# Seven block products for eight in the up-projection of a two-layer encoder trunk, with the down-projection beside them

## The chip, the cores and the metric

The kernel runs on one core of a Trainium2 chip. Its time is the device time of one execution in microseconds (us), taken as the median of three runs. The profile is one further execution, with its own time. The engines are named as in the profile: PE is the matrix engine's multiplication, PEld its loading of the stationary operand, DVE the vector engine, ACT the scalar engine, POOL the GpSimd engine, SP the engine that issues most transfers.

## The reference

The trunk has two layers over 512 tokens of width 1024. Each layer is a mixer (attention or a matrix memory, with an output projection) and then a channel mixer, and this case is about the channel mixers alone:

```python
def causal_dwconv(x, w, b):          # width 3 along the tokens, one filter per channel
    ...
def conv_ffn(h, w_up, conv_w, conv_b, w_down):
    u, g = jnp.split(h @ w_up, 2, axis=-1)
    g = causal_dwconv(g, conv_w, conv_b)
    return (jax.nn.silu(g) * u) @ w_down

x = x + conv_ffn(rmsnorm(x, norm_ffn_g[l]), ffn_w_up[l], ffn_conv_w[l], ffn_conv_b[l], ffn_w_down[l])
```

`w_up` is 1024 x 5632 (an up half and a gate half of 2816 = 22 x 128 columns each), `w_down` is 2816 x 1024. All data are 32-bit floats.

## The kernel before

**Precision.** Every product is made of three matrix multiplications. A value t is split into a high part in the PE's reduced 32-bit format (a cast on ACT, line 129) and a low part t minus high (a subtraction on DVE, line 130). `mm3` (lines 162 to 164) then adds high by high, high by low and low by high in one PSUM bank.

**Layout.** The tokens lie along the free dimension. `xT` is the residual stream: eight tiles of 128 channels x 512 tokens. The input of the channel mixer is `act`, eight pairs (high, low) of `xT` times the norm's gain. The per-token factor of the norm, `norm.row`, is multiplied in afterwards.

**One hidden tile.** `ffn_hidden(l, j, act, norm)` makes hidden tile j of 22. `project` loads the 1024 x 128 weights of the gate (512 KB), splits them, and runs 8 x 3 multiplications of 128x128 by 128x512; the up half has the same. So a tile is 48 multiplications of 512 columns. From the gate's bank, DVE multiplies by the norm's row (line 632), ACT starts the convolution (line 634), DVE adds its other two taps (line 636), ACT applies Silu (line 639), DVE multiplies by the row (line 640) and by the up half (line 644), and the result is split into a pair.

**Chunks.** The 22 tiles come in chunks of 8, 8 and 6 (`CHUNKS`). After each chunk, the down-projection multiplies the chunk's pairs by the rows of `w_down` and adds to the residual (line 951 in layer 0, line 1152 in layer 1): 528 multiplications of 512 columns in a layer. Layer 1 does this part token-major (hidden tile stationary, weights moving), after 32 transposes of `xT` (`token_major`), which stand in its first chunk.

**Order and buffers.** A scheduler sets the order on each engine, save inside a block marked as manual, where PE, ACT and DVE keep the order in which the code is written. Each engine runs its own instructions strictly in order. Tiles come from rings with a number of buffers per tag: `wr`, `wh`, `wl` (raw weights, high and low part) three each, `u` 57, `t` eight, `pt` two; PSUM banks are `mm` three, `sc` three, `tr` two. `xspill` is a copy of the residual in device memory; `reload_x` reads it back.

Of the kernel before, what the change touches and what calls it, by code (L numbers as in the profile page):

```python
# [10 lines left out]
F32R = mybir.dt.float32r  # L11
I32 = mybir.dt.int32
AF = mybir.ActivationFunctionType
ALU = mybir.AluOpType
AX = mybir.AxisListType

P = 128
# [18 lines left out]
    (("fw0", 66), ("fb0", 22)),  # L36
    (("fw1", 66), ("fb1", 22)),
)
CHUNKS = ((0, 8), (8, 16), (16, 22))


def f(ap):
# [4 lines left out]
def trunk(  # L47
# [80 lines left out]
    def split(hi, lo, src, on_act=True, pinned=False):  # L128
        high = A.copy(hi, src) if on_act else V.tensor_copy(hi, src)  # L129
        low = V.tensor_tensor(out=lo, in0=src, in1=f(hi), op=ALU.subtract)  # L130
        if pinned:
            pin(high)
            pin(low)
# [27 lines left out]
    def mm3(o, lh, ll, rh, rl, first, last):  # L161
        nc.tensor.matmul(o, lh, rh, start=first, stop=False)  # L162
        nc.tensor.matmul(o, lh, rl, start=False, stop=False)  # L163
        nc.tensor.matmul(o, ll, rh, start=False, stop=last)  # L164
# [75 lines left out]
    class Norm:  # L240


        def __init__(self):
            self.acc = self.row = None
# [343 lines left out]
    class OutProjection:  # L588
# [30 lines left out]
    def ffn_hidden(l, j, act, norm):  # L619
        w = ffn_w_up[l]  # L620
        fw, fb = col[f"fw{l}"], col[f"fb{l}"]
        gate, up = project(w, DFF + j * P, act), project(w, j * P, act, "sc")
        og = ou = None
        if norm.row is None:
            both = pair_of(gate, up)
            weave(norm.finish(), both, 1)
            og, ou = run(both)
        else:
            og = run(gate)
        pre = sb("t", [P, S + 4])  # L630
        G.memset(pre[:, 0:2], 0.0)
        V.tensor_tensor(out=pre[:, 2 : S + 2], in0=og, in1=norm.row, op=ALU.mult)  # L632
        acc = sb("t", [P, S])
        A.activation(acc, pre[:, 0:S], AF.Identity, scale=fw[:, j : j + 1], bias=fb[:, j : j + 1])  # L634
        for c in (1, 2):
            V.scalar_tensor_tensor(  # L636
                acc, pre[:, c : c + S], fw[:, c * FT + j : c * FT + j + 1], acc, op0=ALU.mult, op1=ALU.add
            )
        A.activation(acc, acc, AF.Silu)  # L639
        V.tensor_mul(acc, acc, norm.row)  # L640
        if ou is None:
            ou = run(up)
        hid = sb("t", [P, S])
        V.tensor_tensor(out=hid, in0=ou, in1=acc, op=ALU.mult)
        hi, lo = sb("u", [P, S], F32R), sb("u", [P, S], F32R)
        split(hi, lo, hid)
        return hi, lo


    def pair(t):  # L650
# [286 lines left out]
    for ci, (j0, j1) in enumerate(CHUNKS):  # L937
        hid = []
        for j in range(j0, j1):
            hid.append(ffn_hidden(0, j, act, norm))  # L940
            if ci and len(reps) < BH:
                bias_rows()
        last = ci == len(CHUNKS) - 1
        if last:
            norm2, kvact, act = Norm(), [], []
        for j in range(KT):
            wh, wl = weights(rows(ffn_w_down[0], j * P, P, j0, j1), j1 - j0, P)
            o = ps("mm")
            for k in range(j1 - j0):
                mm3(o, wh[:, k, :], wl[:, k, :], *hid[k], k == 0, k == j1 - j0 - 1)  # L950
            V.tensor_add(xT[j], xT[j], o)  # L951
            if last:
                norm2.add(xT[j])
                kvact.append(scaled(xT[j], col["gkv"][:, j : j + 1]))
                act.append(scaled(xT[j], col["gmix"][:, 8 + j : 9 + j]))
                G.dma_start(xspill[j], xT[j])
    norm = norm2


# [163 lines left out]
    for ci, (j0, j1) in enumerate(CHUNKS):  # L1123
        hid = []
        for j in range(j0, j1):
            hid.append(ffn_hidden(1, j, act, norm))
            if ci == 0:
                token_major(j % TT, j // TT)
        last = ci == len(CHUNKS) - 1
        n = (j1 - j0) // 2  # L1130
        for hf in range(2):
            os_ = [ps(t) for t in (("mm", "mm", "mm", "sc") if hf == 0 else ("sc", "sc", "tr", "tr"))]
            ws = [None] * n
            groups = [(range(TT), (slice(0, S),))]
            if last and hf:

                groups = [((0, 1), (slice(0, S),)), ((2,), (slice(0, S),)), ((3,), (slice(0, MEM), slice(MEM, S)))]
            for Ts, pieces in groups:
                for c in pieces:
                    if c.start:  # L1140
                        os_[Ts[0]] = ps("mm")
                    for u in range(n):
                        if ws[u] is None:
                            ws[u] = weights(rows(ffn_w_down[1], hf * S, S, j0 + 2 * u, j0 + 2 * u + 2), 2, S)
                        wh, wl = ws[u]
                        for T in Ts:
                            for i in range(2):
                                k = 2 * u + i
                                lh, ll = (t[:, T * P : (T + 1) * P] for t in hid[k])
                                mm3(os_[T][:, c], lh, ll, wh[:, i, c], wl[:, i, c], k == 0, k == j1 - j0 - 1)  # L1150
                    for T in Ts:
                        V.tensor_add(xt[T][hf][:, c], xt[T][hf][:, c], os_[T][:, c])
                        if last:
                            add_squares(T, xt[T][hf][:, c])
                            if hf == 0:
                                V.tensor_mul(xt[T][0], xt[T][0], fgb[0])
                            elif c.stop == S:
                                final_norm(T)


# [44 lines left out]
```

## Time and profile before

| | |
|---|---|
| median of 3 runs | 1232.34 us (1232.07 to 1232.56) |
| profiled execution, its own time | 1232.33 us |
| its span, first to last instruction | 1230.5 us |
| granted PE clock | 0.999 of full speed |
| PE busy | 1219.2 us, 99% of the span |
| PEld busy | 1022.7 us, 83% |
| DVE busy | 807.4 us, 66% |
| ACT busy | 560.5 us, 46% |

The span is 1.8 us shorter than the execution's own time, and the profiled execution agrees with the median to 0.01 us. PE's busy time is the union of the rows of its multiplications; a row begins where the multiplication begins to stream and ends when its last result is through, so rows of successive multiplications overlap. What a multiplication costs in a row of many is therefore the distance between two starts, not the length of a row.

### The profile page before, as it was taken

How to read it: one execution, taken by the hardware profiler on the slowest of the kernel's cores; microseconds unless marked ns; L12 is line 12 of the kernel's file. 1: busy time of each engine (PE TensorE's matmuls, PEld its weight loads, DVE VectorE, ACT ScalarE, POOL GpSimd, SP SyncE). 2: the span in 40 equal slices, each digit the busy share in tenths (PEclk: the TensorE clock that was granted, in tenths of full speed). 3: DMA queues.
4: the chain of work that ended last, by engine and by line, in shares of the span. 5: the costliest groups of instructions: out<-in, count | busy, mean ns of one | idle time of the engine just before them, and what ended most of it. 6: DMA issues, size and time to landing. Idle time of an engine off the chain costs nothing.

```text
span 1230.5 us, 15552 instructions
## 1 busy us (share of the span) xinstructions
PE 1219.2 (99%) x5839; PEld 1022.7 (83%) x5839; DVE 807.4 (66%) x1427; ACT 560.5 (46%) x911; POOL 55.3 (4%) x155
## 2 busy tenths in 40 slices
PE   9999999999999999999999999999999999999997
PEld 8988888888888888888888888888888888888886
DVE  7877687787564466445688888987656255544555
ACT  4546576644332233223365677775334123322334
POOL 1300000000000011000011000000000000000000
PEclk9999999999999999999999999999999999999999
DMA  8634111333344344424263323243232333323321
GB/s 271 210 90 120 53 53 56 116 103 104 103 113 110 104 126 129 125 87 113 77 180 113 93 70 98 61 141 112 88 102 86 103 90 99 103 87 101 103 86 69
DMA packets 190301, 130.63 MB, mean 106 GB/s; under 512 B 6328, under 2 KB 177810, under 8 KB 190226
## 3 DMA queue, kind: packets, MB, share of 16 engines
q1 hardware_dynamic: 186130, 116.59, 31.7%
q0 software_dynamic: 4096, 13.05, 3.8%
q8 instruction: 46, 0.75, 0.3%
q14 instruction: 29, 0.24, 0.1%
HBM read 122.08 MB, written 11.47 MB: 109 GB/s over the span
## 4 chain that ended last, share of the span: by engine, by line
PE 95%; ACT 2%; DVE 1%; DMA 0%; issue 0%; SPq 0%; DVEq 0%; ACTq 0%
PE pmm L162 20%; PE pmm L163 19%; PE pmm L164 19%; PE psc L162 8%; PE psc L163 8%; PE psc L164 8%; PE psc L500 2%; PE ptr L164 1%; PE ptr L162 1%; PE ptr L163 1%; PE ptr L1029 1%; PE ptr L1050 1%; PE ptr L1051 1%; DMA u<-in_mem_dram 0%; PE ptr L569 0%; PE ptr L583 0%
## 5 line engine op out<-in xcount | busy, mean ns | idle before, releaser
L129 ACT CAST wh<-wr 128x1024 fp32r<-128x1024 f32 (+2 forms) x208 | 210.1, 1012 | 432.9 <-issue 178.1
L162 PE MATMUL pmm<-u,wh 128*128 128x512 f32 (+1 forms) x960 | 378.0, 394 | 0.0
L164 PE MATMUL pmm<-u,wl 128*128 128x512 f32 (+1 forms) x960 | 373.9, 390 | 0.0
L163 PE MATMUL pmm<-u,wh 128*128 128x512 f32 (+1 forms) x960 | 373.6, 389 | 0.1
L130 DVE TENSOR_TENSOR wl<-wr,wh 128x1024 fp32r<-128x1024 f32 (+2 forms) x208 | 243.9, 1173 | 98.3 <-ACT wh L129 97.7
L164 PEld LDWEIGHTS pmm<-u,wl 128*128 128x128 f32 x960 | 180.4, 188 | 36.6
L163 PEld LDWEIGHTS pmm<-u,wh 128*128 128x128 f32 x960 | 180.7, 188 | 33.1 <-DVE u L130 0.5
L162 PEld LDWEIGHTS pmm<-u,wh 128*128 128x128 f32 x960 | 180.6, 188 | 32.8
L162 PE MATMUL psc<-u,wh 128*128 128x512 f32 x368 | 143.6, 390 | 0.0
L164 PE MATMUL psc<-u,wl 128*128 128x512 f32 x368 | 143.3, 389 | 0.0
L163 PE MATMUL psc<-u,wh 128*128 128x512 f32 x368 | 143.2, 389 | 0.0
L632 DVE TENSOR_TENSOR t<-pmm,rb 128x512 f32<-128x512 f32 x44 | 30.5, 692 | 116.1 <-PE pmm L164 116.0
L163 PEld LDWEIGHTS psc<-u,wh 128*128 128x128 f32 x368 | 69.1, 188 | 14.2
L162 PEld LDWEIGHTS psc<-u,wh 128*128 128x128 f32 x368 | 69.1, 188 | 14.3
L164 PEld LDWEIGHTS psc<-u,wl 128*128 128x128 f32 x368 | 69.1, 188 | 14.2
L636 DVE SCALAR_TENSOR_TENSOR t<-t,cols,t 128x512 f32<-128x512 f32 x88 | 65.9, 749 | 3.4 <-ACT t L634 1.9
L639 ACT ACTIVATE t<-t 128x512 f32<-128x512 f32 x44 | 27.8, 632 | 83.3 <-DVE t L636 83.3
L951 DVE TENSOR_TENSOR u<-u,pmm 128x512 f32<-128x512 f32 x24 | 16.5, 688 | 56.8 <-PE pmm L164 56.7
L640 DVE TENSOR_TENSOR t<-t,rb 128x512 f32<-128x512 f32 x44 | 30.5, 693 | 29.8 <-ACT t L639 29.8
L162 PE MATMUL pmm<-wh,u 128*128 128x512 f32 (+3 forms) x128 | 45.8, 363 | 1.5 <-ACT wh L129 1.5
L163 PE MATMUL pmm<-wl,u 128*128 128x512 f32 (+3 forms) x128 | 46.0, 360 | 0.0
L164 PE MATMUL pmm<-wh,u 128*128 128x512 f32 (+3 forms) x128 | 45.5, 358 | 0.0
(261 smaller groups left out, 1609.0 us busy)
## 6 DMA issues: line engine op xcount, KB each, us to landing
wr<-in_ffn_w_up_dram SPq DMA_DIRECT2D x88, 512.0 KB, 3.8
wr<-in_ffn_w_down_dram SPq DMA_DIRECT2D x38, 512.0 KB, 3.7
wr<-in_a_w_in_dram SPq DMA_DIRECT2D x20, 512.0 KB, 3.7
wr<-in_w_kv_dram SPq DMA_DIRECT2D x12, 512.0 KB, 3.8
xspill<-u POOLq DMA_DIRECT2D x16, 256.0 KB, 2.6
u<-xspill SPq DMA_DIRECT2D x16, 256.0 KB, 4.8
wr<-in_b_w_in_dram SPq DMA_DIRECT2D x8, 512.0 KB, 4.2
rep<-in_b_rel_row_dram POOLq DMA_DIRECT2D x12, 320.0 KB, 4.7
```

What stands on the lines that cost most here:

```text
L129: high = A.copy(hi, src) if on_act else V.tensor_copy(hi, src)
L130: low = V.tensor_tensor(out=lo, in0=src, in1=f(hi), op=ALU.subtract)
L162: nc.tensor.matmul(o, lh, rh, start=first, stop=False)
L163: nc.tensor.matmul(o, lh, rl, start=False, stop=False)
L164: nc.tensor.matmul(o, ll, rh, start=False, stop=last)
L500: nc.tensor.matmul(o, a, b, start=first and i == 0, stop=i == 1)
L632: V.tensor_tensor(out=pre[:, 2 : S + 2], in0=og, in1=norm.row, op=ALU.mult)
L636: V.scalar_tensor_tensor(acc, pre[:, c : c + S], fw[:, c * FT + j : c * FT + j + 1], acc, op0=ALU.mult, op1=ALU.add)
L639: A.activation(acc, acc, AF.Silu)
L640: V.tensor_mul(acc, acc, norm.row)
L951: V.tensor_add(xT[j], xT[j], o)
L1029: nc.tensor.transpose(tp[:, b * P : (b + 1) * P], es[T, h][:, b * P : (b + 1) * P], ident)
```

## The change

Tiles 0 to 6 of each layer are made as before, apart from tiles 4 to 6, whose input already holds the norm's row and gain. From tile 7 on (`PLAIN`), gate and up half of one tile are one block product:

- The weights of a tile are four blocks: a11 and a12 (up half, first and second half of the 1024 rows), a21 and a22 (gate half). The input is four blocks as well: two halves of the channels by two halves of the tokens (256 columns each).
- Four sums of weight blocks are made per tile on DVE (line 845 of the new code): s1 = a21 + a22, s2 = s1 - a11, s3 = a11 - a21, s4 = a12 - s2. Four sums of input blocks per channel pair are made once in a layer (`forms`). The sums are split into high and low part like everything else.
- Seven products replace eight: a11, a12, a22, s1, s2, s3 and s4, each with one block or sum of the input. A product is 4 x 3 multiplications of 256 columns, so a tile is 84 multiplications of 256 columns. Two banks, r1 and r3, hold partial sums that several outputs share: ACT copies r1 out (lines 796, 802, 812, 819), then PE goes on adding to r1. DVE adds the pieces (lines 799, 813, 895).
- The block for tiles 7 to 21 (`later`, `step`) is a manual order of PE, ACT and DVE. Step j holds the products of tile j, the end of tile j-1 (`Tail`: the taps, Silu, gate times up, the split) and the weight sums and splits of tile j+1 (`Forms`).
- Inside each step up to tile 20, and beside the plain tiles 5 and 6, stand two down-projection products over four hidden tiles each (24 multiplications of 512 columns, lines as `down_products`): ACT copies the result out of PSUM (line 735) and POOL adds it to `xspill` in device memory with an accumulating transfer (line 736). This covers hidden tiles 0 to 15; `reload_x` then brings the residual back, and tiles 16 to 21 (`LAST`) go through the down-projection at the end as in the last chunk before. Both layers now write `xspill` in `OutProjection.finish` (line 619). Layer 1's tiles 0 to 15 are now channel-major, and its 32 transposes stand between the two halves of its last part.

```diff
-CHUNKS = ((0, 8), (8, 16), (16, 22))
+PLAIN, UNSCALED, GROUP, LAST = 7, 4, 4, 6
+H = S // 2
...
                 V.tensor_add(xT[j], xT[j], o)
+                pin(G.dma_start(xspill[j], xT[j]))
...
+        def forms(self):
+            for j in range(KT):
+                V.scalar_tensor_tensor(
+                    xT[j], xT[j], self.gain[:, j : j + 1], self.norm.row, op0=ALU.mult, op1=ALU.mult
+                )
+                hi, lo = sb("u", [P, S], F32R), sb("u", [P, S], F32R)
+                split(hi, lo, xT[j])
...
+        def down_products(self, q, i, w):
+            g, jj = divmod(q, KT // 2)
+            o = ps("tr")
+            c = slice(i * P, (i + 1) * P)
+            for k in range(GROUP):
+                mm3(o, w[0][:, k, c], w[1][:, k, c], *self.hid[GROUP * g + k], k == 0, k == GROUP - 1)
+            return 2 * jj + i, o
+        def add(self, j, o):
+            t = sb("t", [P, S])
+            A.copy(t, o)
+            G.dma_start(xspill[j], t, accum_op=ALU.add)
...
+        def products(self, o, w, act, first=False):
+            n = KT // 2
+            for k in range(n):
+                mm3(o[:, :H], w[0][:, k], w[1][:, k], *act[k], first and k == 0, k == n - 1, True)
...
+        def step(self, j, w, nxt, tail):
+            new = Tail(self, j)
+            then(tail, "last_block", "first_tap")
+            w.split_fourth()
+            r1, r2, new.r3 = ps("mm"), ps("mm"), ps("sc")
+            new.up, new.u3, new.pre = sb("t", [P, S]), sb("t", [P, S]), sb("t", [P, S])
+            self.products(r1, w.a11, self.b(0, 0), True)
+            A.copy(new.up[:, :H], r1[:, :H])
+            then(tail, "second_tap")
+            self.products(r2, w.a12, self.b(1, 0), True)
+            V.tensor_tensor(out=new.up[:, :H], in0=new.up[:, :H], in1=r2[:, :H], op=ALU.add)
+            then(tail, "third_tap")
+            self.products(r1, w.s2, self.t(2))
+            A.copy(new.up[:, H:], r1[:, :H])
+            then(nxt, "sums")
+            then(tail, "gated")
+            then(nxt, "split_second", "sum_third")
+            w.down_products(0)
+            self.products(new.r3, w.s1, self.t(1), True)
+            w.add_down(0)
+            then(tail, "split")
+            then(nxt, "split_up")
+            self.products(r1, w.s3, self.t(3))
+            A.copy(new.u3[:, :H], r1[:, :H])
+            V.tensor_tensor(out=new.pre[:, H:], in0=new.u3[:, :H], in1=new.r3[:, :H], op=ALU.add)
+            then(nxt, "split_sums")
+            w.down_products(1)
+            then(nxt, "sum_fourth")
+            w.add_down(1)
+            self.products(r1, w.a22, self.t(4))
+            A.copy(new.pre[:, :H], r1[:, :H])
+            then(nxt, "split_down", "split_gate")
+            self.products(new.r3, w.s4, self.b(1, 1))
```

The prediction speaks of two places in the program. The first is ACT in the steady part of layer 0. Before, one hidden tile (`wh` are cast weights, `t` the convolution, `u` the hidden tile's high part; the names in brackets are the engines or transfers waited for):

```order
L129 CAST wh_4452<-wr_4450 128x1024 [waits DMAHW2_49,PE_49,Activation_49]
L634 ACTIVATE t_4364<-t_4361,cols_783 128x512 [waits DVE_49,Pool_49]
L639 ACTIVATE t_4364<-t_4364 128x512 [waits DVE_49]
L129 CAST wh_4492<-wr_4490 128x1024 [waits DMAHW3_49,PE_49,Activation_49]
L129 CAST u_4403<-t_4401 128x512 [waits DVE_49]
```

After, from the last copy of r1 in one step into the next step:

```order
L819 COPY t_4591<-pmm_4586 128x256 [waits PE_49]
L133 CAST wh_4726<-wr_4577 128x1024 [waits DMAHW7_49]
L133 CAST u_4730<-pt_3326 128x512 [waits DMAHW6_49]
L652 ACTIVATE t_4755<-t_4591,cols_783 128x512 [waits DVE_49,Activation_49]
L133 CAST u_4757<-pt_3327 128x512 [waits DVE_49]
L796 COPY t_4764<-pmm_4761 128x256 [waits PE_49]
L907 ACTIVATE t_4755<-t_4755 128x512 [waits DVE_49,Activation_49]
L802 COPY t_4764<-pmm_4761 128x256 [waits PE_49]
L133 CAST u_4812<-pt_3327 128x512 [waits DVE_49]
L735 COPY t_4842<-ptr_4817 128x512 [waits PE_49]
```

Between two copies of r1 there are now casts of the next tile's weights and sums (lines 133) and the last tile's convolution (line 652), in one queue.

The second place is PE, where the third product (s2, in `u_4637`) follows the second (a12) into r1 (`pmm_4761`), and then POOL, with the accumulating transfers:

```order
L169 MATMUL pmm_4762<-u_3322,wl_4675 128x256
L167 MATMUL pmm_4761<-u_3365,u_4637 128x256 [waits Activation_49]
L168 MATMUL pmm_4761<-u_3366,u_4637 128x256
L169 MATMUL pmm_4761<-u_3365,u_4638 128x256
L167 MATMUL pmm_4761<-u_3415,u_4637 128x256
```

The product s2 waits for ACT's copy of r1 (line 796, above); before, a bank was not added to again after it had been read.

```order
L1220 DMA rep_4746<-in_b_rel_row_dram 128x640
L1222 DMA rep_4746<-maskf 64x64 [waits DMASW2_49,DMASW1_49]
L736 DMA xspill<-t_4842 128x512 [waits DMASW3_49,Activation_49]
L736 DMA xspill<-t_4885 128x512 [waits DMASW4_49,Activation_49]
L1220 DMA rep_4921<-in_b_rel_row_dram 128x640
L1222 DMA rep_4921<-maskf 64x64 [waits DMASW6_49,DMASW5_49]
```

In layer 0 the two accumulating transfers of a step stand in POOL's queue between the two transfers that prepare layer 1's bias rows, which stood between the hidden tiles before as well.

More of the change, by code (lines that the diff above doesn't have):

```diff
@@ L159, in rows, with mm3 @@
         return w[k0 * P : k1 * P, c0 : c0 + n].rearrange("(k p) c -> p k c", p=P)
[L161 to L164, printed above, removed]
+    def mm3(o, lh, ll, rh, rl, first, last, more=False):
+        nc.tensor.matmul(o, lh, rh, start=first, stop=False, skip_group_check=more)
+        nc.tensor.matmul(o, lh, rl, start=False, stop=False, skip_group_check=more)
+        nc.tensor.matmul(o, ll, rh, start=False, stop=last, skip_group_check=more)
     def project(w, c0, act, tag="mm"):
@@ L617, in finish @@
             return norm, acts
[L619 to L637, printed above, removed]
-            )
[L639 to L647, printed above, removed]
@@ new lines, in trunk, with __init__, halves, form @@
+    class Forms:
+        def __init__(self, mixer, j):
+            self.mixer, n = mixer, KT // 2
+            self.q = j - GROUP - 1
+            self.up, self.gate = mixer.load_pair(j)
+            self.raw_down = mixer.load_down(self.q) if self.q < 4 * n else None
+            self.s13 = mixer.s[:, :D].rearrange("p (a b) -> p a b", a=KT)
+            self.s24 = mixer.s[:, D : 2 * D].rearrange("p (a b) -> p a b", a=KT)
+        def halves(self, t):
+            n = KT // 2
+            return t[:, :n], t[:, n:]
+        def form(self, src):
+            hi, lo = (sb("u", [P, S], F32R).rearrange("p (a b) -> p a b", a=KT // 2) for _ in range(2))
+            split(hi, lo, src)
+            return hi, lo
+        def sub(self, o, x, y, op=ALU.subtract):
+            V.tensor_tensor(out=o, in0=x, in1=y, op=op)
+        def sums(self):
+            a21, a22 = self.halves(self.gate)
+            s1, s2 = self.halves(self.s13)[0], self.halves(self.s24)[0]
+            self.sub(s1, a21, a22, ALU.add)
+            self.sub(s2, s1, self.halves(self.up)[0])
+        def split_second(self):
+            self.s2 = self.form(self.halves(self.s24)[0])
+        def sum_third(self):
+            self.sub(self.halves(self.s13)[1], self.halves(self.up)[0], self.halves(self.gate)[0])
+        def split_up(self):
+            self.a11, self.a12 = zip(*(self.halves(t) for t in parts(self.up)))
+        def split_sums(self):
+            self.s1, self.s3 = zip(*(self.halves(t) for t in parts(self.s13)))
+        def sum_fourth(self):
+            s2, s4 = self.halves(self.s24)
+            self.sub(s4, self.halves(self.up)[1], s2)
+        def split_down(self):
+            if self.raw_down is not None:
+                self.down = parts(self.raw_down)
+        def split_gate(self):
+            self.a22 = self.form(self.halves(self.gate)[1])
+        def split_fourth(self):
+            self.s4 = self.form(self.halves(self.s24)[1])
+        def down_products(self, i):
+            if self.raw_down is not None:
+                self.o = self.mixer.down_products(self.q, i, self.down)
+        def add_down(self, i):
+            if self.raw_down is not None:
+                self.mixer.add(*self.o)
@@ new lines, in trunk, with __init__, last_block, first_tap @@
+    class Tail:
+        def __init__(self, mixer, j):
+            self.mixer, self.j = mixer, j
+        def last_block(self):
+            c = self.up[:, H:]
+            V.tensor_tensor(out=c, in0=c, in1=self.r3[:, :H], op=ALU.add)
+        def first_tap(self):
+            self.acc = sb("t", [P, S])
+            self.mixer.last_tap(self.j, self.acc, self.pre)
+            self.taps = self.mixer.taps(self.j, self.acc, self.pre)
+        def second_tap(self):
+            next(self.taps)
+        def third_tap(self):
+            next(self.taps)
+            A.activation(self.acc, self.acc, AF.Silu)
+        def gated(self):
+            V.tensor_tensor(out=self.acc, in0=self.up, in1=self.acc, op=ALU.mult)
+        def split(self):
+            self.mixer.keep(self.acc)
@@ new lines, in channel_mixer @@
+    def channel_mixer(l, act, norm, gain, beside):
+        mixer = ChannelMixer(l, act, norm, gain, beside)
+        forms = mixer.forms()
+        run(mixer.plain(0))
+        for j in range(1, UNSCALED):
+            weave(mixer.plain(j), forms, KT / (16.0 * (UNSCALED - 1)))
+        until(lambda: len(mixer.ready) == KT, forms) if len(mixer.ready) < KT else None
+        mixer.buffers()
+        for j in range(UNSCALED, PLAIN):
+            q = j - GROUP - 1
+            raw = mixer.load_down(q) if q >= 0 else None
+            weave(mixer.plain(j), forms, 4 / (16.0 * 2))
+            if raw is not None:
+                w = parts(raw)
+                for i in range(2):
+                    mixer.add(*mixer.down_products(q, i, w))
+        run(forms)
+        mixer.later()
+        reload_x()
+        return mixer.hid[FT - LAST :]
@@ L935, in bias_rows, with more_rows @@
         reps.append(rep)
[L937 to L956, printed above, removed]
+    def more_rows():
+        if len(reps) < BH:
+            bias_rows()
+    hid = channel_mixer(0, act, norm, col["gffn"][:, 0:8], more_rows)
+    norm2, kvact, act = Norm(), [], []
+    for j in range(KT):
+        wh, wl = weights(rows(ffn_w_down[0], j * P, P, FT - LAST, FT), LAST, P)
+        o = ps("mm")
+        for k in range(LAST):
+            mm3(o, wh[:, k, :], wl[:, k, :], *hid[k], k == 0, k == LAST - 1)
+        V.tensor_add(xT[j], xT[j], o)
+        norm2.add(xT[j])
+        kvact.append(scaled(xT[j], col["gkv"][:, j : j + 1]))
+        act.append(scaled(xT[j], col["gmix"][:, 8 + j : 9 + j]))
+        G.dma_start(xspill[j], xT[j])
     norm = norm2
@@ L1121, in final_norm @@
         nc.sync.dma_start(out[T * P : (T + 1) * P, S:], xt[T][1])
[L1123 to L1150, printed above, removed]
-                    for T in Ts:
[L1152 to L1158, printed above, removed]
```

138 lines of the change are left out of this document (added).

## The prediction

> **What bounds the kernel now.** I read the page's head and busy times first, then the chain that ended last, then PE alone in the two channel mixers.
>
> ```profile
> span 1230.5 us, 15552 instructions
> PE 1219.2 (99%) x5839; PEld 1022.7 (83%) x5839; DVE 807.4 (66%) x1427; ACT 560.5 (46%) x911; POOL 55.3 (4%) x155
> PE 95%; ACT 2%; DVE 1%; DMA 0%; issue 0%; SPq 0%; DVEq 0%; ACTq 0%
> ```
>
> PE is 99% busy and is 95% of the chain. That alone does not say that PE waits nowhere, since its rows overlap. So I asked for the channel mixers apart: first the groups of PE in the stretch from 300 to 600 us (layer 0), then the busy times of all engines in a piece of each layer's mixer.
>
> ```profile
> L162 PE MATMUL pmm<-u,wh 128*128 128x512 f32 x282 | 109.7, 389 | 0.0
> L163 PE MATMUL psc<-u,wh 128*128 128x512 f32 x160 | 62.2, 389 | 0.0
> ...
> 300.00:400.00 100.00, 100.00 (x443) 82.82 (x442) 55.95 (x67) 33.62 (x41) 4.00 (x13) 1.00 0.38 107
> 900.00:1000.00 100.00, 100.00 (x453) 82.78 (x452) 47.68 (x56) 30.68 (x38) 0.50 (x5) 1.00 0.31 94
> ```
>
> The last column of a group is PE's idle time before it: 0.0. In the window rows come PE, PEld, DVE, ACT and POOL with their counts, then PE's clock (1.00). DVE has 56 us of work in 100, ACT 34. So the mixers are PE's stream of multiplications and nothing else; what counts is how many there are and how far apart they start. The timeline of PE at the end of the kernel shows both widths in one loop, with nothing waiting:
>
> ```profile
> 1213.25 0.39 PE L163 MATMUL psc<-wl,u 128*128 128x512 f32 x1
> ...
> 1218.92 0.39 PE L164 MATMUL ptr<-wh,u 128*128 128x512 f32 x1
> 1219.14 0.28 PE L162 MATMUL ptr<-wh,u 128*128 128x256 f32 x1
> 1219.26 0.28 PE L163 MATMUL ptr<-wl,u 128*128 128x256 f32 x1
> ...
> 1223.22 0.28 PE L163 MATMUL pmm<-wl,u 128*128 128x256 f32 x1
> ```
>
> The first and the second row of 512 columns stand 25 starts apart: 5.67 us / 25 = 226.8 ns. (The window of layer 0 says the same: 443 rows touch its 100 us, of which two began before it: 100 / 441 = 226.8.) From 1219.14 to 1223.22 there are 34 starts of 256 columns: 4.08 / 34 = 120.0 ns. So half the columns cost 53% of the time, not 50%: about 13 ns of each multiplication do not shrink with its width. This is the tax on the change.
>
> **The change, part by part.** *The products.* A tile before is 48 x 226.8 = 10.89 us. A tile now is 84 x 120.0 = 10.08 us. By columns alone seven eighths would save 1.36 us; the fixed 13 ns of 36 more multiplications take back about 0.5. The gain is 0.81 us a tile, and 15 tiles in 2 layers make 30: **24.2 us**.
>
> Each multiplication has a weight load of its own, and there will be 36 more in a tile:
>
> ```profile
> L164 PEld LDWEIGHTS pmm<-u,wl 128*128 128x128 f32 x960 | 180.4, 188 | 36.6
> ```
>
> A load's row is 188 ns, longer than the 120.0 ns between two narrow multiplications, so loads run beside multiplications. One rule of the Trainium skill speaks against that: "TensorE: Matmul & The Clock Gate", section "The mechanism" of the part on packing, says that a weight load overlaps a multiplication in flight only where the two use different row groups, and here all use all rows. By that rule the loads would stand in line, and more and narrower multiplications would lose, as in the third rival; the trace does not agree with it (188 ns against 120.0).
>
> *The down-projection.* 16 tiles go through 16 x 2 products of 12 x 2 multiplications: 8 x 16 x 3 = 384 a layer, and the last six 144. That is 528 as before, all of 512 columns. In layer 1 weights and hidden tiles change roles; both orders show 0.39 us rows at 227 ns. Nothing.
>
> *What DVE and ACT get.* The durations:
>
> ```profile
> L130 DVE TENSOR_TENSOR wl<-wr,wh 128x1024 fp32r<-128x1024 f32 x178 | 217.9, 1224 | 89.4 <-ACT wh L129 89.0
> L130 DVE TENSOR_TENSOR u<-t,u 128x512 fp32r<-128x512 f32 x62 | 42.5, 686 | 2.2 <-ACT u L129 2.0
> L636 DVE SCALAR_TENSOR_TENSOR t<-t,cols,t 128x512 f32<-128x512 f32 x88 | 65.9, 749 | 3.4 <-ACT t L634 1.9
> L130 DVE TENSOR_TENSOR u<-pmm,u 128x256 fp32r<-128x256 f32 x12 | 5.1, 421 | 1.0 <-ACT u L129 0.9
> L129 ACT CAST wh<-wr 128x1024 fp32r<-128x1024 f32 x178 | 187.2, 1053 | 403.9 <-issue 172.8 <-PE pmm L163 115.1 <-PE psc L163 39.7
> L129 ACT CAST u<-t 128x512 fp32r<-128x512 f32 x62 | 38.1, 615 | 5.7 <-DVE t L520 3.9 <-DVE t L644 1.5
> L634 ACT ACTIVATE t<-t,cols 128x512 f32<-128x512 f32 x44 | 36.0, 817 | 9.4 <-DVE t L632 9.0 <-issue 0.2
> L639 ACT ACTIVATE t<-t 128x512 f32<-128x512 f32 x44 | 27.8, 632 | 83.3 <-DVE t L636 83.3
> L129 ACT CAST u<-pmm 128x256 fp32r<-128x256 f32 x12 | 4.5, 374 | 5.2 <-DVE u L130 5.1
> L1094 ACT COPY u<-ptr 128x512 f32<-128x512 f32 x8 | 4.6, 579 | 0.0
> ```
>
> A step is 84 x 120.0 + 24 x 226.8 = 15.52 us of PE. DVE has in it three low parts of 1024 (3.67), nine operations of 512 (four sums, four low parts, the gating: 6.17), two taps (1.50) and three additions of 256 (1.26): 12.6 us, 81%. ACT has three casts of 1024, four of 512, two activations, four copies of 256 and two of 512: 3.16 + 2.46 + 1.45 + 1.50 + 1.16 = 9.7 us, 63%. The sums of DVE do not appear in the trace by name; I price them by the 512 row, the same operation between SBUF tiles. Both engines fit, so PE hides them as long as their order hands PE each operand in time.
>
> *The new waits inside a step.* PE now adds to r1 after ACT has copied it, four times a step. The tightest is the product s2. After r1's last product (a22) PE has s4, a11 and a12 before s2: 3 x 1.44 = 4.32 us. In that time ACT must do what the order shows: copy 0.374, cast of the down weights 1.053, cast of a22 0.615, first tap 0.817, cast of s4 0.615, copy of r1 0.374: 3.85 us. The first copy starts when the last row ends, 0.28 - 0.12 = 0.16 us after its place in the stream. So 0.31 us of room are left if nothing overlaps. In the trace ACT's instructions overlap by about 0.09 us where they follow each other:
>
> ```profile
> 299.80 1.05 ACT L129 CAST wh<-wr 128x1024 fp32r<-128x1024 f32 x1 [2.11 <-issue]
> 300.76 0.61 ACT L129 CAST u<-t 128x512 fp32r<-128x512 f32 x1
> 301.28 0.82 ACT L634 ACTIVATE t<-t,cols 128x512 f32<-128x512 f32 x1
> ```
>
> (299.80 + 1.05 is 0.09 after 300.76.) Five such overlaps give 0.45 us, so the room is 0.3 to 0.75 us; some 0.04 us for each of two semaphores come off. The other waits have more: the copy before the second use of a down bank or of r1 has a down product of 24 / 2 x 0.2268 = 2.72 us of cover, against 0.37 + 0.16. I take zero here, and 0.3 us a step as the bad end.
>
> *The sums of the input.* They are made once a layer beside plain tiles 1 to 6. In tiles 1 to 3 DVE has 8 x (0.749 + 0.686) = 11.5 us of them beside 3 x 6.7 of its own work (two low parts of 1024, four operations of 512, two taps), 31.6 us in 3 x 10.89 = 32.7. In tiles 4 to 6 it loses the two multiplications by the row and gains four groups of 4 x 0.421 + 2 x 0.686, some 31 us in 43. The first stretch is 97% full; weights are split up to three tiles ahead, so I take 0, and 2 us a layer as the bad end.
>
> *Edges.* Tile 21's tail runs after its last product: copy, tap, two taps, Silu, gating, split, 0.37 + 0.82 + 1.50 + 0.63 + 0.69 + 0.62 + 0.69 = 5.3 us from the end of a22, of which 1.44 lie beside s4; the other 3.9 lie beside down products of tiles 16 to 20 (15 multiplications, 3.4 us, for each output tile). About 0.4 us a layer. In layer 1 the 32 transposes are copied out by ACT, eight copies of 0.579 us from two banks, at one place instead of one copy per tile: up to 0.7 us. Sum: **+1.5 us**.
>
> *Transfers.* The weights are the same bytes. New are 64 accumulating transfers of 256 KB, and the residual is loaded twice more. The trace has neither an accumulating transfer nor its price; the nearest are
>
> ```profile
> xspill<-u POOLq DMA_DIRECT2D x16, 256.0 KB, 2.6
> u<-xspill SPq DMA_DIRECT2D x16, 256.0 KB, 4.8
> ```
>
> so 2.6 us from below, 7.4 from above, if the read and the write of the old value simply follow each other. What they must meet: the buffer of a step's second sum is asked for again a step later, by ACT's copy of the same kind, so from the end of that copy 15.52 - 0.58 - 0.55 (POOL's issue) = 14.4 us. I take 7.4, hidden. The reload stands behind the last of them by the step of tile 21, which has no down product (84 x 0.12 = 10.1 us).
>
> Sum: -24.2 + 1.5 = **-22.7 us**, against the profiled execution's 1232.3: **1209.6 us**, which the median of the runs equals.
>
> **The rivals.**
>
> 1. *ACT's queue binds.* The copy of r1 comes late and s2 waits, each step, 0.3 us: 30 x 0.3 = 9 us, so 1218 to 1219; with the full first stretch on DVE, 4 us more. For it: the 0.3 us of room without overlap. Against it: the overlap in the rows above.
> 2. *Accumulating transfers are slow (slower than before).* Where one takes longer than 14.4 us, ACT's copy waits for its buffer, the copies behind it in ACT's queue wait too, and PE with them. Every further us costs 1 us in each of 30 steps, so from 14.4 + 22.7 / 30 = 15.2 us on the kernel is slower; at 17 us it is -22.7 + 2.6 x 30, or 1288 us. Against it: twice the upper bound. For it: no row shows this kind of transfer, and the two in a step share POOL's queue with the bias rows.
> 3. *The weight load binds.* Were the 188 ns of a load the spacing of narrow multiplications, a tile would take 84 x 0.188 = 15.8 us, 30 x 4.9 = 147 us more than before, 1379 us. Against it: 120.0 ns in the last 35 multiplications, in the same helper.
>
> 4. *The gain is given back whole*: PE waits some 0.8 us in every step for several operands together. Nothing in the sums of DVE (81%) or ACT (63%) asks for it; 1230 to 1234.
>
> **How the numbers follow.** What a measurement of this kernel tells from no change is about 0.2%, 2.5 us. My forecast (1206 to 1213) has 0.72; the first rival (1213 to 1222) 0.15; the fourth 0.03; the second 0.08; the third 0.01; 0.01 is left for less than 1206, which no term allows. Faster is then 0.88, the same 0.03, slower 0.09. The range must leave out no more than 2 in 10 and goes from 1205 to 1220.
>
> **What would show it.** Narrow multiplications 120 ns apart inside a step and steps 15.5 us apart: the main term. No idle time of PE before the first multiplication of s2 (line 167, from r1's copy): the room in ACT's queue. Landing of the accumulating transfers (line 736) under 14 us. DVE near 13 us and ACT near 10 in each step. PE's idle time at the two layer ends under 1 us each. The prediction is wrong if the narrow multiplications spread when each waits for a different engine, or if the transfers into device memory queue up.

## The result, and the profile after

The changed kernel takes 1211.51 us (median of 4 runs, 1210.64 to 1212.10) against 1232.30 us before: a ratio of 0.9831 with a 95% interval of 0.9814 to 0.9848. The forecast was 1209.6 us.

The page's head of the changed kernel, in the form of the one before:

```profile
span 1210.3 us, 18434 instructions
PE 1197.6 (99%) x6919; PEld 1054.6 (87%) x6919; DVE 934.3 (77%) x1703; ACT 693.0 (57%) x1217; POOL 115.7 (10%) x191
PE 92%; ACT 3%; DVE 3%; issue 0%; DMA 0%; SPq 0%; DVEq 0%; ACTq 0%
```

PE has 1080 multiplications more and is 21.6 us less busy; DVE and ACT took over 127 and 133 us of new work, and PE still bounds the kernel. A window inside layer 0's steps (columns: PE, PEld, DVE, ACT, POOL with counts, PE's clock, share of the transfer engines, GB/s):

```profile
440.00:540.00 100.00, 100.00 (x690) 93.42 (x690) 75.62 (x110) 56.67 (x96) 18.47 (x25) 1.00 0.69 156
```

DVE is 76% busy, ACT 57%. The list of PE's waits has no row between the start and the end of the steps. So the time is again the distances of starts. PE's timeline through one product of 256 columns, one down product and the first start behind it:

```profile
467.90 0.28 PE L167 MATMUL pmm<-u,u 128*128 128x256 f32 x1
...
469.22 0.28 PE L169 MATMUL pmm<-u,u 128*128 128x256 f32 x1
469.34 0.40 PE L167 MATMUL ptr<-u,wh 128*128 128x512 f32 x1
469.57 0.40 PE L168 MATMUL ptr<-u,wh 128*128 128x512 f32 x1
...
470.50 0.39 PE L169 MATMUL ptr<-u,wl 128*128 128x512 f32 x1
...
472.08 0.28 PE L167 MATMUL psc<-u,wh 128*128 128x256 f32 x1
...
483.46 0.28 PE L167 MATMUL pmm<-u,u 128*128 128x256 f32 x1
```

The narrow product takes 1.44 us for 12 starts, 120.0 ns each, as at the end of the kernel before. The first five starts of the wide product take 1.16 us (469.34 to 470.50), 232 ns each; the other seven take 1.58 us, 226 to 227 ns each. The wide multiplications behind a narrow run thus start a little slower, 0.02 to 0.03 us in all for each switch, and a step has two. The last row is the product s2 of the next step, 15.56 us after the first row.

To compare the kernels stage by stage, I took the starts of DVE's last additions to the residual as marks, in each output projection and in layer 0's down-projection, and for the end of layer 1's mixer the start of PE's last multiplication. The marks of mixer 0, first before and then after:

```profile
282.23 0.69 DVE L613 TENSOR_TENSOR u<-u,pmm 128x512 f32<-128x512 f32 x1 [2.05 <-PE pmm L164]
642.70 0.69 DVE L951 TENSOR_TENSOR u<-u,pmm 128x512 f32<-128x512 f32 x1
...
283.37 0.69 DVE L618 TENSOR_TENSOR u<-u,pmm 128x512 f32<-128x512 f32 x1 [2.05 <-PE pmm L169]
633.09 0.69 DVE L1236 TENSOR_TENSOR u<-u,pmm 128x512 f32<-128x512 f32 x1
```

The stages (us):

| | head (to the end of layer 0's output projection) | channel mixer 0 | between | channel mixer 1 | distance of two steps |
|---|---|---|---|---|---|
| before | 282.23 | 360.48 | 216.39 | 364.24 | |
| after | 283.37 | 349.72 | 216.54 | 353.50 | 15.56 |

Each channel mixer became 10.75 us shorter. The head is 1.1 us longer; all that the change adds there are POOL's writes of the residual to `xspill` at its end.

### The profile page after: what moved, and what is told of

It is laid out like the page before. It is cut to its first block, busy times and chain, and to the rows that moved or that the text cites. A ratio compares the mean times of both kernels' runs of the same rounds, so it can differ in the third digit from the quotient of the medians.

```text
span 1210.3 us, 18434 instructions
## 1 busy us (share of the span) xinstructions
PE 1197.6 (99%) x6919; PEld 1054.6 (87%) x6919; DVE 934.3 (77%) x1703; ACT 693.0 (57%) x1217; POOL 115.7 (10%) x191
## 3 DMA queue, kind: packets, MB, share of 16 engines
q0 software_dynamic: 14592, 34.03, 14.4%
## 4 chain that ended last, share of the span: by engine, by line
PE 92%; ACT 3%; DVE 3%; issue 0%; DMA 0%; SPq 0%; DVEq 0%; ACTq 0%
PE pmm L167 17%; PE pmm L169 17%; PE pmm L168 17%; PE ptr L167 6%; PE ptr L168 6%; PE ptr L169 6%; PE psc L167 6%; PE psc L169 6%; PE psc L168 6%; PE psc L505 2%; PE ptr L1313 1%; PE ptr L1334 1%; PE ptr L1335 1%; ACT wh L133 1%; DMA u<-in_mem_dram 0%
## 5 line engine op out<-in xcount | busy, mean ns | idle before, releaser
L167 PE MATMUL pmm<-u,wh 128*128 128x512 f32 (+1 forms) x952 | 336.0, 353 | 0.1
L168 PE MATMUL pmm<-u,wh 128*128 128x512 f32 (+1 forms) x952 | 332.2, 349 | 0.1
L134 DVE TENSOR_TENSOR wl<-wr,wh 128x1024 fp32r<-128x1024 f32 (+4 forms) x178 | 206.9, 1163 | 119.6 <-ACT wh L133 118.8
L133 ACT CAST wh<-wr 128x1024 fp32r<-128x1024 f32 (+4 forms) x178 | 178.4, 1004 | 131.6 <-PE pmm L168 50.3
L167 PE MATMUL ptr<-u,wh 128*128 128x512 f32 x272 | 106.7, 392 | 0.0
L168 PE MATMUL ptr<-u,wh 128*128 128x512 f32 x272 | 106.5, 392 | 0.0
L169 PE MATMUL ptr<-u,wl 128*128 128x512 f32 x272 | 105.8, 389 | 0.0
L736 POOL DMA_DIRECT2D xspill<-t x64 | 55.6, 868 | 472.6 <-ACT t L735 462.2
L167 PE MATMUL psc<-u,wh 128*128 128x512 f32 (+1 forms) x248 | 84.0, 339 | 0.0
L169 PE MATMUL psc<-u,wl 128*128 128x512 f32 (+1 forms) x248 | 83.8, 338 | 0.0
L168 PE MATMUL psc<-u,wh 128*128 128x512 f32 (+1 forms) x248 | 83.8, 338 | 0.0
L169 PE MATMUL pmm<-u,u 128*128 128x256 f32 x264 | 74.9, 284 | 0.2 <-DVE u L134 0.2
L167 PE MATMUL pmm<-u,u 128*128 128x256 f32 x264 | 75.0, 284 | 0.0
L168 PE MATMUL pmm<-u,u 128*128 128x256 f32 x264 | 74.8, 283 | 0.0
L134 DVE TENSOR_TENSOR u<-pt,u 128x512 fp32r<-128x512 f32 x90 | 61.7, 689 | 5.1 <-ACT u L133 3.0
```

The source lines that it names most:

```text
L167: nc.tensor.matmul(o, lh, rh, start=first, stop=False, skip_group_check=more)
L168: nc.tensor.matmul(o, lh, rl, start=False, stop=False, skip_group_check=more)
L169: nc.tensor.matmul(o, ll, rh, start=False, stop=last, skip_group_check=more)
L736: G.dma_start(xspill[j], t, accum_op=ALU.add)
```

## The experiments

### How much belongs to the seven products: where they begin

The first three kernels change one number, the first tile of seven products. With 20, two tiles a layer are left, and nearly all else of the change stands alone. A time without a number of runs, here and below, is that of a single run.

```diff
-PLAIN, UNSCALED, GROUP, LAST = 7, 4, 4, 6
+PLAIN, UNSCALED, GROUP, LAST = 20, 4, 4, 6      # 6 and 14 in the others
...
         for j in range(UNSCALED, PLAIN):
             q = j - GROUP - 1
+            if j >= 7:
+                beside()                         # not with 6
```

> The seven products begin at tile 6 instead of 7: two tiles more. My theory (each tile made of seven products saves 48 x 226.8 - 84 x 120.0 = 0.81 us of the matrix engine, less 0.04 us a step that the changed kernel's steps are longer than their products): 2 x 0.77 = 1.5 us less, 1210.0 us. Rival (the vector engine is full before the steps begin): tiles 4 and 5 would hold four groups of input sums (12.2 us), their own 2 x 5.3, one down weight's low part (1.2) and the first step's weight sums and splits (7.8), 31.8 us in 2 x 10.89 + 5.44 = 27.2 us of the matrix engine, less some 2 us by overlap; the matrix engine then waits some 2.5 us in each layer, 1214 to 1215 us.

> The seven products begin at tile 14: 8 tiles a layer instead of 15, while the down-projection stays beside the tiles in groups of four (the bias rows of layer 1 are made beside the plain tiles from 7 on too). My theory (the gain is 0.77 us for each tile of seven products and nothing else): 14 x 0.77 = 10.8 us more than the changed kernel, 1222.3 us. Rival (part of the gain comes from the new down-projection, through which the residual's additions leave the vector engine): less than half of that, 1216 us or under.

> The seven products begin at tile 20: two tiles a layer; all else as in the changed kernel, so this is almost the other half of the change alone. My theory: 26 x 0.77 = 20.0 us more than the changed kernel, 1231.5 us, and on the line through the other two. Rival (the new down-projection gives part of the gain): clearly under 1228 us. Second rival (the new down-projection costs more than the 1.5 us that I gave the edges): 1234 us or more.

| first tile of seven products | median us (runs) | ratio to before, 95% | mixer 0 | mixer 1 | tiles of seven in a layer |
|---|---|---|---|---|---|
| 20 | 1230.87 (10) | 0.9988 (0.9979 to 0.9998) | 359.58 | 363.34 | 2 |
| 14 | 1223.96 (4) | 0.9927 (0.9912 to 0.9942) | 355.02 | 358.81 | 8 |
| 7 (the change) | 1211.51 (4) | 0.9831 (0.9814 to 0.9848) | 349.72 | 353.50 | 15 |
| 6 | 1209.36 (4) | 0.9813 (0.9798 to 0.9828) | 348.93 | 352.70 | 16 |

The mixers lie on a line: from 2 to 15 tiles mixer 0 loses 9.86 us and mixer 1 9.84, which is 0.758 us a tile. That is close to the 0.81 of the products less the 0.04 that a step is longer than its products. The three forecasts miss by 0.6 to 1.7 us. Carried on to no tile at all, the line gives 359.58 + 2 x 0.758 = 361.10 us, 0.62 more than before, and in mixer 1 364.86, also 0.62 more. So the other half of the change, the down products beside the tiles and the additions in device memory, gives nothing of the gain; it costs 0.6 us a layer. The rivals of all three fall.

Tile 6 works too: 0.79 us less in each mixer. The sum by which DVE would have been too full fell here. It set 31.8 us of DVE's work, less 2 by overlap, against 27.2 us from the start of tile 4 to the first step. The trace has DVE busy for 26.0 us in that stretch (columns as in the window further up):

```profile
326.90:354.30 27.40, 27.40 (x122) 22.69 (x121) 26.01 (x44) 17.09 (x27) 0.89 (x1) 1.00 0.34 97
```

So DVE is nearly full, but the work fits. Part of what was counted lies outside the stretch: the sums of the first of the four groups of input sums begin at 322.47, before tile 4, and a low part of 1024 columns (1.2 us) begins at 355.36, after the first start of the step at 354.31.

### What the down products do beside the tiles

They bring no gain of their own, so I left them out of the steps.

```diff
-            self.raw_down = mixer.load_down(self.q) if self.q < 4 * n else None
+            self.raw_down = None
```

> The down products of the steps are left out (tiles 7 to 20, weights, multiplications and additions), so the output lacks their part; the steps hold the seven products alone. What counts is the distance of two steps. If the matrix engine is the only bound: 84 x 0.120 = 10.1 us. My theory: the down products are the cover under which the other engines work; without them the vector engine has 12.6 - 1.2 = 11.4 us of work in a step (10.1 to 11.4 with overlap), and the copy of the shared bank after the product s3 has nothing before the product a22 to hide under (0.37 + 0.16 + 0.04 = 0.57 us of waiting). So 10.7 to 12 us a step, most likely 11.2, with the waits at a22 and at the operands that the vector engine makes.

The kernel takes 1089.89 us. Steps are 11.20 us apart, 1.1 more than the 84 starts take. The largest entry in the list of PE's waits (columns: us in total, times, longest us):

```profile
PE pmm L167 <- ACT t L812: 19.8, 28, 0.7
```

One of these 28 places, in PE's timeline and then in ACT's:

```profile
457.88 0.28 PE L169 MATMUL pmm<-u,wl 128*128 128x256 f32 x1
458.88 0.38 PE L167 MATMUL pmm<-u,u 128*128 128x256 f32 x1 [0.73 <-ACT t L812]
459.11 0.28 PE L168 MATMUL pmm<-u,u 128*128 128x256 f32 x1
...
457.52 1.04 ACT L133 CAST wh<-wr 128x1024 fp32r<-128x1024 f32 x1
458.47 0.36 ACT L812 COPY t<-pmm 128x256 f32<-128x256 f32 x1
```

Here the product a22 starts 1.00 us after the last multiplication of s3 instead of 0.12, for ACT copies the shared bank (line 812) in between, and the multiplication after that comes 0.22 us later, not 0.12. The most likely 11.2 us was met, but not by the terms of its sum. The wait at a22 was put at 0.57 us and is 0.88: s3's last row ends at 458.16, and ACT begins the copy 0.31 us later, at 458.47, behind a cast of weights in its queue. For operands that DVE makes the sum left about 0.5 us, and the trace shows 0.15 us, at s4. So the hit is in part luck. DVE is 89% busy in this kernel:

```profile
440.00:540.00 100.00, 94.19 (x755) 91.39 (x754) 89.46 (x140) 60.33 (x107) 0.55 (x1) 1.00 0.33 90
```

The down products are cover: without them the same seven products would take 11.20 us and not 10.08, more than the 10.89 us of the tile before. So in this order of the products the change needs both halves, though only one of them pays; another order of the seven products, without down products, was not tried.

### The room in ACT's queue

```diff
+            G.memset(self.raw[:, 2 * D :], 0.0)                       # once a layer
...
+            for _ in range(2):                                       # one in the first kernel
+                A.copy(self.s[:, 2 * D :], self.raw[:, 2 * D :])
             A.copy(new.up[:, :H], r1[:, :H])
```

> One needless copy of 512 columns on the scalar engine (from and to spare columns; 0.615 us, 0.53 with overlap) ahead of the copy of the shared bank before the product s2, in every step; the vector engine and the transfers are untouched. In the trace of the changed kernel that copy ends 0.79 us before s2 begins. My theory (that room is real): steps stay 15.56 us apart, the time stays within 2 us of the changed kernel's 1211.5. Rival (the matrix engine reads its semaphore early, or the room is used by something the trace does not show): steps grow by up to 0.5 us, 15 us in all.

> Two such copies, 1.06 us with overlap. My theory: 1.06 - 0.75 = 0.31 us are missing in each step, the first multiplication of s2 waits for the scalar engine, steps 15.85 to 15.9 us apart, 30 x 0.31 = 9 us in all, about 1221 us. Rival (the scalar engine, 63% busy, has room to spare): no change.

With one copy the steps stay 15.56 us apart and the time is 1210.54 us. With two they are 16.09 us apart and the time is 1224.45 us. So the room is real, and of ACT's copies it is the tightest place (in the changed kernel's step above, the copies before s3 and a22 end 2.1 us or more before PE needs them), but I had sized the second copy too small. ACT's timeline of that kernel:

```profile
468.02 1.27 ACT L798 COPY pt<-pt 128x512 f32<-128x512 f32 x2
469.20 0.37 ACT L799 COPY t<-pmm 128x256 f32<-128x256 f32 x1
```

PE's timeline at the same place:

```profile
469.06 0.28 PE L169 MATMUL pmm<-u,wl 128*128 128x256 f32 x1
469.62 0.39 PE L167 MATMUL pmm<-u,u 128*128 128x256 f32 x1 [0.28 <-ACT t L799]
469.85 0.28 PE L168 MATMUL pmm<-u,u 128*128 128x256 f32 x1
```

The second copy follows the first without overlap, so the two move the next copy by 1.18 us and not by 1.06 (468.02 to 469.20). It writes where the first wrote; whether that is the reason no run shows. Against 0.75 us of room, 0.43 are missing, and PE's start is 0.56 us after the one before instead of 0.12, so 0.44. Another 0.10 us follow: the next start comes after 0.23 us.

### The additions in device memory

```diff
-            G.dma_start(xspill[j], t, accum_op=ALU.add)
+            G.dma_start(xspill[j], t)                    # first kernel: writes
...
+            for _ in range(1 + 2 * (j % 2)):             # second kernel: the second sum, three times
+                G.dma_start(xspill[j], t, accum_op=ALU.add)
```

> The 64 transfers into device memory write instead of adding, so the output lacks sums of the down-projection. My theory (the accumulating transfers are hidden, 4.6 us to landing against 14.4 us of room): steps and time as in the changed kernel, 15.56 us and 1211.5 within 2 us; the landing falls from 4.6 to about 2.6 to 3 us. Rival (adding in device memory slows other transfers and with them the steps): faster by more than 2 us.

> The second of the two additions of a step is issued three times, one after the other has landed (so the output holds it three times). Its buffer is then held for three issues and landings, 3 x (0.87 + 4.6) = 16.4 us, against the 14.4 to 15.0 us after which the scalar engine asks for it again. My theory (the slower rival's mechanism is real, and its point lies there): steps of 16.5 to 17.5 us in layer 1, more in layer 0, where the bias rows (6 us) stand in the same queue; 1240 to 1300 us. Rival (the buffers give more room than I counted): 15.56 us and no change.

In the changed kernel, an addition lands 4.6 us after its issue:

```profile
xspill<-t POOLq DMA_DIRECT2D x64, 256.0 KB, 4.6
```

With plain writes it is 2.8 us, within what was expected:

```profile
xspill<-t POOLq DMA_DIRECT2D x64, 256.0 KB, 2.8
```

The mixers then take 349.74 and 353.48 us, steps are 15.56 us apart and the time is 1210.45 us, so the additions are hidden whole.

With the second sum added three times, the time is 1255.24 us, but only layer 0 pays: mixer 0 takes 394.24 us, mixer 1 353.46, with 15.56 us a step as if nothing had happened. The expectation for layer 1 was wrong. In this program the buffer is asked for again by the first tap (line 652) two steps on and not by the next copy of its kind, which leaves some 18 us from the end of the copy. In layer 0, steps are 16.4 to 21.6 us apart from the second on. PE's, ACT's and POOL's waits in layer 0's mixer:

```profile
PE pmm L167 <- ACT t L797: 29.3, 11, 4.3
ACT t L652 <- DMA xspill<-t: 31.5, 9, 5.1
POOL xspill L737 <- DMA xspill<-t: 129.0, 31, 6.1
POOL rep L1223 <- DMA rep<-in_b_rel_row_dram: 75.6, 12, 7.6
```

POOL waits in its own queue for each addition and for the bias rows, so the third addition of a step is issued too late and ACT's tap waits for its buffer, up to 5.1 us. The copy of r1 (line 797 here) stands behind that tap in ACT's queue, and PE waits for it, 29.3 us in all.

The other third of layer 0's 44.5 us is PE's clock. The first row below is the stretch of the waits as a whole (columns as in the window further up), with a mean clock of 0.94; then come one wait in PE's timeline and PE alone behind it (PE, its clock, share of the transfer engines, GB/s):

```profile
407.00:623.00 216.00, 189.26 (x1208) 174.08 (x1209) 134.97 (x196) 100.18 (x170) 53.60 (x68) 0.94 0.77 154
...
616.11 0.28 PE L169 MATMUL pmm<-u,wl 128*128 128x256 f32 x1
618.28 0.39 PE L167 MATMUL pmm<-u,u 128*128 128x256 f32 x1 [1.90 <-ACT t L797]
...
619.30:622.60 3.30, 3.30 (x12) 0.50 0.48 104
```

There are eight such stretches of 3.4 us at half clock, each at the end of one of the eleven waits or shortly behind it. They cost 8 x 3.4 / 2 = 13.6 us; with 29.3 us of waiting and about 0.1 us behind each wait that makes 44.0. The mechanism of the slower rival exists; the point from which it decides is set by POOL's queue in layer 0, and in layer 1 three landings do not reach it.

### Where the early start stops paying

Last, I ran the change and the version from tile 6 side by side, and the version from tile 5.

> The changed kernel once more, beside the next one on the same chip, to weigh the two against each other: 1211.5 us within 1.5. The time before its channel mixers was 283.4 us in its first profile against 281.9 to 282.5 in five of the others, whose code is the same up to there; if that is chance, the profile of this run shows about 282.2 there.

> The seven products from tile 6 on, once more: 0.77 us less in each layer than the changed kernel, 1.5 us in all, 0.9987 of its time. If the first measurement's 2.1 us was chance and the vector engine costs something after all: the same time.

> The seven products from tile 5 on. By the products alone another 1.5 us less than from tile 6, 1207.8 us. My theory (the vector engine sets how early the steps can begin): tile 4 alone (10.9 us of the matrix engine) must cover its own 5.3 us of vector work, the four groups of input sums (12.2) and the first step's first sums and low parts (about 4.0), 21.5 us, less 2 us by overlap; the matrix engine waits 4 to 8 us in each layer, 1216 to 1224 us, with its waits on the vector engine at the first step.

The change takes 1211.77 us (4 runs; 0.9829, 0.9815 to 0.9842), the version from tile 6 1209.26 us (5 runs; 0.9810, 0.9797 to 0.9823), beside 1232.54 us before (9 runs) on the same chip. The intervals touch; what settles it is the mixers, 348.93 and 352.70 us in both profiles of the version from tile 6, against 349.71 and 353.47. It is the fastest of those that leave nothing out, by 0.8 us a layer.

From tile 5 the time is 1224.15 us. PE waits at the first step of each layer, first for ACT's copy, then for DVE:

```profile
341.40 0.28 PE L169 MATMUL pmm<-u,wl 128*128 128x256 f32 x1
345.02 0.58 PE L167 MATMUL pmm<-u,u 128*128 128x256 f32 x1 [3.34 <-ACT t L796]
345.40 0.42 PE L168 MATMUL pmm<-u,u 128*128 128x256 f32 x1
347.22 0.58 PE L169 MATMUL pmm<-u,u 128*128 128x256 f32 x1 [1.40 <-DVE u L134]
347.60 0.41 PE L167 MATMUL pmm<-u,u 128*128 128x256 f32 x1
347.81 0.41 PE L168 MATMUL pmm<-u,u 128*128 128x256 f32 x1
...
349.52 0.63 PE L167 MATMUL ptr<-u,wh 128*128 128x512 f32 x1
349.95 0.63 PE L168 MATMUL ptr<-u,wh 128*128 128x512 f32 x1
```

Windows before, in and behind these waits (columns as in the window further up):

```profile
330.00:341.00 11.00, 11.00 (x59) 9.48 (x58) 10.10 (x22) 7.40 (x12) 0.00 (x0) 1.00 0.15 49
341.40:345.00 3.60, 0.28 (x3) 0.07 (x1) 3.60 (x7) 3.06 (x6) 0.00 (x0) 0.94 0.00 0
345.00:348.40 3.40, 1.98 (x7) 1.69 (x8) 3.40 (x6) 0.00 (x0) 0.00 (x0) 0.50 0.30 86
348.40:351.80 3.40, 3.40 (x14) 2.94 (x13) 2.68 (x5) 0.92 (x2) 0.00 (x0) 0.56 0.78 222
```

DVE is the engine that is full here: busy for all 7.00 us of the second and third window, of which PE is busy 2.26. ACT's copy (line 796), for which PE waits first, stands in ACT's queue behind casts that had to wait for DVE's input sums. So DVE does set how early the steps can begin, one tile earlier than I had first put it. The granted clock is 0.50 behind the first wait, and starts are about 210 and 430 ns apart in place of 120 and 227. Half clock lasted 6.8 us: 0.43 of the second window by its mean of 0.94, all 3.40 of the third, 2.99 of the fourth by its 0.56. "TensorE: Matmul & The Clock Gate" of the Trainium skill, section "What's actually happening", says that an idle window of about 3.4 us halves PE's clock; the trace agrees, with 3.6 us between two starts and half clock after them. The kernel with three additions shows that less can do: there half clock also followed waits of 1.9 to 2.5 us (four of them), while two of 2.1 and 2.3 us had none behind them.

## Why the prediction was right

**The products.** The forecast was 0.81 us a tile and 24.2 in all. Measured are 0.758 and 22.7. The two distances were right to the nanosecond, 120.0 and 227. What was missing is the switch: a step was put at 15.52 us and takes 15.56, since each of its two down products begins with five slower starts. Over the 28 steps that have down products this is 1.1 us of the missing 1.5, and I had priced narrow and wide multiplications only from runs of one kind.

**The down-projection and the edges.** The count of 528 is right, though "16 x 2 products of 12 x 2" is a slip: they are 32 products of 12 multiplications, 384. "Nothing" for 528 equal multiplications and +1.5 us for the edges: the line through the three starts leaves 2 x 0.62 = 1.2 us. Of it, the trace has 0.37 us of late starts at the end of tile 21 in layer 0, and 0.56 us between the transposes of layer 1; the rest was not traced.

**The waits inside a step.** The room before s2 was put at 0.3 to 0.75 us. In the trace ACT's copy ends at 467.11 (466.74 + 0.37):

```profile
466.74 0.37 ACT L796 COPY t<-pmm 128x256 f32<-128x256 f32 x1
```

The product s2 starts at 467.90, in the first row of PE's timeline shown above. So it was the upper end, 0.75 us after the semaphore's 0.04; the overlap of ACT's instructions holds in this order too. One needless copy fits in, two do not. The first rival had the right place and was not reached.

**DVE and ACT.** Forecast 12.6 and 9.7 us a step; the window gives 0.756 x 15.56 = 11.8 and 0.567 x 15.56 = 8.8, lower because overlapped time counts once: the rows of a step add up to 12.6 and 9.7.

**The input sums.** "0, with 2 us as the bad end": PE waits nowhere there, with 7 or with 6 as the first tile.

**The transfers.** 4.6 us lies between the bounds of 2.6 and 7.4. The reading behind the room of 14.4 us was wrong, as the third addition showed: the buffer's next user is the first tap two steps on, not the next copy of its kind. It changed nothing here, since either room is far above 4.6 us.

**The sum.** Both mixers together became 21.5 us shorter against 22.7 forecast: the products gave 1.5 less, mostly by the switches, and the edges cost 0.3 less. The medians differ by 20.8. The rest lies most likely in the head: it took 281.9 to 284.6 us in the thirteen profiles, twelve of them with the same code there. In some of them a transfer of the first inputs comes later, in some PE runs at half clock for one stretch of 3.4 us; the second profile of the changed kernel had 283.87 us there, 1.5 us of it in such a stretch. Why the changed kernel's two profiles both lie above the middle is open.

The rivals of weight loads and of a whole gain given back are out: the load's row is 190 ns after the change, and the narrow starts of a tile still stand 120.0 ns apart.

## What to carry to other kernels

A block scheme that saves an eighth of the columns is worth what the spacing of starts says, not the eighth: here 13 ns a multiplication do not shrink with its width, and 12.5% fewer columns became 7% less time for a tile. Such a scheme also puts copies between products on one bank, so in the order used here it needs other products as cover; count for each shared bank what stands in the copying engine's queue between one use and the next, with the overlap that the trace shows, and put work of another kind between. How early it can begin is set by the engine that prepares its operands, and the last tile that fits is found by trying the one before.

## What was not expected of the hardware

- Behind a run of 256-column multiplications the first five of 512 columns start 232 ns apart, not 226.7.
- A narrow multiplication that had to wait costs about 0.1 us beyond its wait: in the kernel without the down products and in the one with two copies the next one starts 0.23 us after it instead of 0.12; at half clock, from tile 5, it is 0.38 instead of 0.21.
- In the version from tile 5, 3.6 us between two starts of PE were followed by half clock for 6.8 us. Its waits in layer 0's first step sum to 4.7 us (3.34 and 1.40), and mixer 0 is 6.7 us longer than in the version from tile 6 (355.64 against 348.93).
- In the kernel with three additions, half clock of 3.4 us followed waits of PE as short as 1.90 us; the eight stretches cost layer 0 about 13.6 us beside the 29.3 us of the waits.
- An addition in device memory (256 KB) lands 4.6 us after its issue, against 3.0 for the plain writes of the same size in the same profile and 2.8 for the same transfers as plain writes, and POOL's row for issuing it is 0.87 us long.
